# Hybrid encoder on one core: two column blocks of the output projection take the delta net's chunks first, and three scalings in the mixer run on ScalarE

## The chip, the core and the metric

The kernel runs on one core of a Trainium2 chip. The metric is the device time of one execution in microseconds (us), as the median of several runs. Each run's time covers the span from the first to the last instruction and a little around it.

## What is computed

Two layers of a bidirectional encoder on 256 tokens of width 2048, all in float32. A layer is a token mixer and a SwiGLU feed-forward net, each between two RMSNorms:

```python
h = rmsnorm(x, pre_mix_norm)
proj = h @ w_in                            # 2048 -> 4176 columns, for three groups
o_a = mla_mixer(...)                       # 8 heads of softmax attention, 1024 columns
o_b = conformer_conv(...)                  # GLU, depthwise conv of width 31, LayerNorm, swish, 512 columns
o_c = gdn_mixer(...)                       # gated delta net, 4 heads, two directions, 512 columns
mix = jnp.concatenate([o_a, o_b, o_c], axis=-1) @ w_out
x = x + rmsnorm(mix, post_mix_norm)
h = rmsnorm(x, pre_ffn_norm)
x = x + rmsnorm((silu(h @ w_gate) * (h @ w_up)) @ w_down, post_ffn_norm)
```

In `mla_mixer` the softmax weights are `exp(s - max) / sum`. In `gdn_mixer` the chunked delta rule multiplies the rows of several 128x128 matrices by gate values, one value for each row.

## The kernel before

Every large product is made from two float32r halves of each operand (`hilo`: the high half is a cast on ScalarE, line 333, and the low half a subtraction on VectorE, line 334). `dense` runs one product: for each 128-row chunk of the weights and each of the two token tiles it issues three matmuls of 512 columns (lines 358 to 360) into a PSUM bank named `acc`; there are four such banks, two for each product. It walks over units of two chunks. A unit loads 512 KB of weights through SP's queue into `ws` (5 buffers), splits them into `wh` and `wl` (5 buffers each), and then has twelve matmuls. At the end `evac` empties the two banks.

All small work of the mixer is background: attention of four head pairs (`attend`), the delta net (`gdn`), the convolution (`conformer`) and others are Python generators. After each unit `bg.step(1.6)` lets them go on; each step of a generator tells its cost at `yield`, and a unit's budget is 1.6. All but the convolution advance at most once in a unit. `bg.ensure` runs a generator to its end on the spot where a product needs its result. What is traced in this order is then put into each engine's queue by a planner, which fills an engine's gaps with later work that it takes to be ready. The 248 products of the depthwise convolution on VectorE (lines 951 and 954, one for each tap and each 128 channels, two layers) are such filling work. Each engine runs its own queue strictly in order.

The output projection has 16 chunks of rows: 0 to 7 are attention's (`oaT`), 8 to 11 the convolution's (`obT`), 12 to 15 the delta net's (`ocT`). It has four blocks of 512 columns. It runs in two passes, with the partial sums kept in SBUF between them:

```python
a, b = list(range(8)), [12, 13, 14, 15, 8, 9, 10, 11]
passes = [[a[:6], a, a, a], [a[6:] + b, b, b, b]]
```

So in the second pass block 0 takes chunks 6 and 7, then the delta net's four, and then at once the convolution's four. `need_mix` makes the convolution's generator end before its first chunk.

The end of the convolution is a chain: eight transposes of its sums (line 961), LayerNorm on VectorE (lines 964 to 969), eight transposes back (line 978), swish on ScalarE (line 983), and the split into halves (lines 333 and 334). The end of the delta net is eight transposes (line 918) and a split with a gain (lines 337 and 338).

The three scalings that change are: `kd` in `gdn_prep` (line 678, the delta net's keys by a gate), `vw` in `gdn_head` (lines 827 and 855, twice for each head and direction) and the division of the softmax weights by their sum in `attend` (line 1043, ahead of the transposes of line 1048). In `attend` the sum is inverted on VectorE (line 1041), after the exponentials on ScalarE (line 1037).

Of the kernel before, what the change touches and what calls it, by code (L numbers as in the profile page):

```python
# [9 lines left out]
F32 = mybir.dt.float32  # L10
# [6 lines left out]
P = 128  # L17
# [41 lines left out]
def kernel(  # L59
# [27 lines left out]
    def v3(ap, a):  # L87
        return ap.rearrange("p (a b) -> p a b", a=a)
# [250 lines left out]
                                 op0=ALU.mult, op1=ALU.subtract)  # L339
        return ins  # L340

    def dense(lhs, ks, n, load, evac, ch=2, need=None, pre=None, head=0, mid=None, tail=0,
              after0=None):

        acc = [psa.tile([P, 512], F32, tag="acc", name="acc") for _ in range(NT)]
        nu = -(-len(ks) // ch)
        held = []  # L350

        def mm(t, c, u, kc, wh, wl):
            i = u * ch + c
            rh = wh[:, c * n:(c + 1) * n]
            rl = wl[:, c * n:(c + 1) * n]
            xh, xl = lhs(kc[c], t)
            o = acc[t][:, 0:n]
            pe.matmul(o, xh, rh, start=(i == 0), stop=False)  # L358
            pe.matmul(o, xl, rh, start=False, stop=False)  # L359
            pe.matmul(o, xh, rl, start=False, stop=(i == len(ks) - 1))  # L360

        def unit(u):
            kc = ks[u * ch:(u + 1) * ch]
            m = len(kc)
            ws = wpool.tile([P, 1024], F32, tag="ws", name="ws", bufs=WSB)
            wv = ws[:, 0:m * n].rearrange("p (c n) -> p c n", c=m)
            load(wv, kc[0], m)
            wh = wpool.tile([P, 1024], F32R, tag="wh", name="wh", bufs=WHB)
            wl = wpool.tile([P, 1024], F32R, tag="wl", name="wl", bufs=WHB)
            with ExitStack() as order:  # L370
                if u < head:
                    for u0, ins in hold:
                        if u >= u0:
                            order.enter_context(tc.issue_after(ins.ins))
                hilo(wh[:, 0:m * n], wl[:, 0:m * n], ws[:, 0:m * n])
            if need is not None:
                for k in kc:
                    bg.ensure(*need(k))
            return u, kc, wh, wl

        for u in range(nu):
            a = unit(u)
            if head <= u < nu - tail:
                for c in range(len(a[1])):
                    for t in range(NT):
                        mm(t, c, *a)
            else:
                for c in range(len(a[1])):
                    mm(0, c, *a)
                held.append(a)  # L390
                if u == head - 1 and mid is not None:
                    mid()
                if u == nu - 1:
                    if pre is not None:
                        pre()
                        pre = None
                    evac(0, acc[0][:, 0:n])
                if u in (head - 1, nu - 1):
                    for h in held:
                        for c in range(len(h[1])):  # L400
                            mm(1, c, *h)
                    held.clear()
            bg.step(BUDGET)
        if pre is not None:
            pre()
        if after0 is not None:
            after0()
        for t in range(1 if tail else 0, NT):
            evac(t, acc[t][:, 0:n])

    def wload(w, n0, n):
# [102 lines left out]
    for l in range(DEPTH):  # L514
# [148 lines left out]
        def gdn_prep():  # L663

            nss = SM(16, "nss")
            kd, vk = [U(), U()], [U(), U()]
            for t in range(NT):
                for i, tl in enumerate((qT, kT)):
                    ps = TP()
                    junk = U()  # L670
                    for h in range(GH):
                        pe.transpose(ps[:, h * P:(h + 1) * P], hsl(tl, h, t), ident)
                    for h in range(GH):
                        j = i * 8 + t * 4 + h
                        act.activation(out=junk[:, h * P:(h + 1) * P], in_=ps[:, h * P:(h + 1) * P],
                                       func=AF.Square, accum_out=nss[:, j:j + 1])
                    if i:
                        dve.tensor_tensor(out=v3(kd[t], 4), in0=v3(ps, 4), in1=bc(G["eg5"][:, t, 1, t], 2, P),
                                          op=ALU.mult)
                    yield 0.4  # L680
            rn = rsqrt(nss, 1.0, EPS, 16, "rn")
            rk = rn[:, 8:16]

            b2, inr = SM(16, "b2"), SM(8, "inr")
            b24 = b2.rearrange("p (t d h) -> p t d h", t=NT, d=2)
            rk2 = SM(8, "rk2")
            dve.tensor_tensor(out=rk2, in0=rk, in1=rk, op=ALU.mult)
            dve.tensor_tensor(out=b24, in0=G["be4"], in1=bc(v3(rk2, NT), 2, 2), op=ALU.mult)
            dve.scalar_tensor_tensor(out=inr, in0=nss[:, 8:16], scalar=EPS, in1=rk, op0=ALU.add, op1=ALU.mult)
            nege = SM(8, "nege")  # L690
            for t in range(NT):
                dve.tensor_scalar(out=nege[:, t * 4:t * 4 + 4], in0=G["eg5"][:, 1 - t, 0, t], scalar1=-1.0,
                                  scalar2=None, op0=ALU.mult)
            yield 2.0

            for t in range(NT):
                ps = TP()
                for h in range(GH):
                    pe.transpose(ps[:, h * P:(h + 1) * P], hsl(vT, h, t), ident)
                dve.tensor_tensor(out=v3(vk[t], 4), in0=v3(ps, 4), in1=bc(inr[:, t * 4:t * 4 + 4], 2, P),  # L700
                                  op=ALU.mult)
                yield 0.7
            G.update(rn=rn, b24=b24, nege=nege, kd=kd, vk=vk)
# [72 lines left out]
        def gdn_head(h):  # L776
# [47 lines left out]
                m = 2 * (1 - d) + d  # L824
                pe.matmul(ps[:, d * P:(d + 1) * P], R[:, m * P:(m + 1) * P], vk[d][:, hs], start=True, stop=True)
            for d in range(2):
                dve.tensor_scalar(out=vw[:, d * P:(d + 1) * P], in0=ps[:, d * P:(d + 1) * P],
                                  scalar1=G["b24"][:, d, d, h:h + 1], scalar2=None, op0=ALU.mult)
            yield 0.4
            ps = TP()  # L830
            for d in range(2):
                pe.matmul(ps[:, d * P:(d + 1) * P], kd[d][:, hs], vw[:, d * P:(d + 1) * P], start=True, stop=True)
# [19 lines left out]
                pe.matmul(ps[:, d * P:(d + 1) * P], R[:, m * P:(m + 1) * P], S[:, (2 + d) * P:(3 + d) * P],  # L852
                          start=True, stop=True)
            for d in range(2):
                dve.tensor_scalar(out=vw[:, (2 + d) * P:(3 + d) * P], in0=ps[:, d * P:(d + 1) * P],
                                  scalar1=G["b24"][:, 1 - d, d, h:h + 1], scalar2=None, op0=ALU.mult)
            yield 0.4
            ps = TP()
            for t in range(NT):
                for d in range(2):  # L860
# [132 lines left out]
        def attend(hp, qn, kv):  # L993
# [28 lines left out]
            def head(i):  # L1022
# [17 lines left out]
                yield 0.8  # L1040
                dve.reciprocal(out=sm, in_=sm)
                for t in range(NT):
                    dve.tensor_scalar(out=pr[:, t * 256:(t + 1) * 256], in0=pr[:, t * 256:(t + 1) * 256],
                                      scalar1=sm[:, t:t + 1], scalar2=None, op0=ALU.mult)
                ps = TP()
                for kt in range(NT):
                    for t in range(NT):
# [1 line left out]
                                     pr[:, t * 256 + kt * P:t * 256 + (kt + 1) * P], ident)  # L1049
                pT = U()  # L1050
                act.copy(out=pT, in_=ps)
                yield 0.5
                ps = TP()
                for kt in range(NT):
                    pe.matmul(ps[:, 0:256], kv[kt][:, i * 256 + P:(i + 1) * 256],  # L1055
# [134 lines left out]
        def out_proj(lhs, passes, w, wpm, rname, need, after0):  # L1190
            parts = {}
            ssqp = [SM(4, "ssqp0"), SM(4, "ssqp1")]
            for i, ks in enumerate(passes):
                last = i == len(passes) - 1
                for nb in range(4):
                    if i == 0:
                        parts[(nb, 0)], parts[(nb, 1)] = U(), U()

                    def ev(t, ps):
                        o = parts[(nb, t)]  # L1200
                        if not last:
                            act.copy(out=o, in_=ps)
                            return
                        if i > 0:
                            dve.tensor_tensor(out=o, in0=o, in1=ps, op=ALU.add)
                            ps = o
                        junk = U()
                        act.activation(out=junk, in_=ps, func=AF.Square, accum_out=ssqp[t][:, nb:nb + 1])

                        def weigh():  # L1210
                            dve.tensor_tensor(out=o, in0=ps, in1=wpm[nb], op=ALU.mult)
                        if nb == 3:
                            residual(t, parts, ssqp, rname, weigh)
                        else:
                            weigh()
                    dense(lhs, ks[nb], 512, wload(w, nb * 512, 512), ev, need=need,
                          **(dict(tail=TAILG, after0=after0) if last and nb == 3 else {}))


        a, b = list(range(8)), [12, 13, 14, 15, 8, 9, 10, 11]  # L1220
        passes = [[a[:6], a, a, a], [a[6:] + b, b, b, b]]
        h2, F = {}, {}
        out_proj(lmix, passes, w_out[l], wpm, "rm", need_mix, lambda: norm_quad(0, 0, h2, (l, PRE_FFN)))

# [399 lines left out]
```

## Time and profile before

| what | value |
|---|---|
| runs before | median 2221.38 us of three (2218.79 to 2222.61) |
| the profiled execution, its own time | 2217.84 us |
| its span | 2216.0 us |
| PE (TensorE matmul) busy | 2183.0 us, 99% |
| DVE (VectorE) busy | 1916.4 us, 86% |
| ACT (ScalarE) busy | 1233.3 us, 56% |
| HBM read over the span | 402.94 MB, 183 GB/s |

The times of all rows are those of the profiled execution, and its own time lies 1.84 us above its span. In the profile a matmul is shown longer than the step from one matmul to the next, since matmuls are pipelined; so a gap between two matmuls of less than some 0.15 us shows as busy.

### The profile page before, as it was taken

The page shows a single profiled execution, that of the slowest core. Times are in us where ns is not written, and L with a number is a line of the kernel's source. Part 1 is how long each engine was busy: PE and PEld are TensorE (multiplying, and loading weights), DVE is VectorE, ACT ScalarE, POOL GpSimd, SP SyncE. Part 2 cuts the span into 40 slices and gives each one's busy share as a digit, 9 for nine tenths or more (in the row PEclk, how much of TensorE's full clock was granted, in tenths as well). Part 3 has the DMA queues.
Part 4 walks back from the last instruction along what each step waited for, and adds up shares of the span by engine and source line. Part 5 has one row for each costly group of instructions (what it writes and reads, how often), then busy time and mean ns, then how long its engine had stood idle before and what let it go on. Part 6 is the DMA issues. An engine that isn't in the chain of part 4 may idle for free.

```text
span 2216.0 us, 29534 instructions
## 1 busy us (share of the span) xinstructions
PE 2183.0 (99%) x10399; PEld 1823.9 (82%) x10399; DVE 1916.4 (86%) x3149; ACT 1233.3 (56%) x1726; POOL 45.7 (2%) x93
## 2 busy tenths in 40 slices
PE   8999999999999999999999999999999999999998
PEld 6988887788888888888879888877888888888886
DVE  6787998899989988889787779979998998988896
ACT  6665545555555555655556655455555555565553
POOL 2000000000000000000000000000000000000000
PEclk9999999999999999999999999999999999999999
DMA  7554534556655656466656545244556556564564
GB/s 252 172 182 144 186 104 153 162 171 199 212 196 200 210 198 225 154 208 211 200 181 184 181 142 175 96 154 162 189 192 227 188 194 226 188 211 161 203 218 148
DMA packets 218547, 407.76 MB, mean 184 GB/s; under 512 B 17607, under 2 KB 30065, under 8 KB 218400
## 3 DMA queue, kind: packets, MB, share of 16 engines
q1 hardware_dynamic: 215360, 397.72, 54.1%
q0 software_dynamic: 3008, 8.16, 1.4%
q8 instruction: 81, 1.33, 0.2%
q14 instruction: 66, 0.54, 0.1%
q10 hardware_dynamic: 32, 0.01, 0.0%
HBM read 402.94 MB, written 2.90 MB: 183 GB/s over the span
## 4 chain that ended last, share of the span: by engine, by line
PE 92%; DVE 5%; DMA 1%; ACT 1%; issue 0%; SPq 0%; DVEq 0%; ACTq 0%; POOLq 0%
PE acc L1398 19%; PE tp L1398 19%; PE tp L1525 10%; PE acc L1525 10%; PE acc L359 9%; PE acc L360 9%; PE acc L358 9%; DVE wl L334 1%; DVE xs L501 1%; PE acc L1246 1%; DMA ws<-in_w_in_dram 1%; PE tp L1055 0%; DMA cd<-u 0%; PE tp L808 0%; PE tp L801 0%; PE tp L1026 0%
## 5 line engine op out<-in xcount | busy, mean ns | idle before, releaser
L333 ACT CAST wh<-ws 128x1024 fp32r<-128x1024 f32 (+3 forms) x848 | 826.8, 997 | 742.5 <-DVE ws L1365 279.4
L334 DVE TENSOR_TENSOR wl<-ws,wh 128x1024 fp32r<-128x1024 f32 (+3 forms) x848 | 956.9, 1154 | 177.1 <-ACT wh L333 164.7
L358 PE MATMUL acc<-wh,u 128*128 128x512 f32 (+2 forms) x1088 | 419.7, 387 | 3.9 <-ACT u L333 3.4
L360 PE MATMUL acc<-wl,u 128*128 128x512 f32 (+2 forms) x1088 | 412.3, 380 | 5.3 <-DVE wl L334 5.1
L359 PE MATMUL acc<-wh,u 128*128 128x512 f32 (+2 forms) x1088 | 412.8, 380 | 1.4 <-DVE u L338 0.7
L1398 PE MATMUL acc<-wh,u 128*128 128x512 f32 x1220 | 376.3, 389 | 0.0
L1398 PE MATMUL tp<-wh,u 128*128 128x512 f32 x1220 | 375.8, 389 | 0.0
L1398 PEld LDWEIGHTS acc<-wh,u 128*128 128x128 f32 x1220 | 228.7, 188 | 47.8 <-DVE u L334 0.6
L1398 PEld LDWEIGHTS tp<-wh,u 128*128 128x128 f32 x1220 | 228.9, 188 | 47.5
L360 PEld LDWEIGHTS acc<-wl,u 128*128 128x128 f32 x1088 | 205.4, 189 | 42.1 <-DVE wl L334 7.7
L358 PEld LDWEIGHTS acc<-wh,u 128*128 128x128 f32 x1088 | 205.6, 189 | 40.1 <-ACT u L333 4.9
L359 PEld LDWEIGHTS acc<-wh,u 128*128 128x128 f32 x1088 | 205.7, 189 | 39.9 <-DVE u L338 3.4
L1398 PE MATMUL acc<-wl,u 128*128 128x512 f32 x610 | 237.3, 389 | 0.0
L1398 PE MATMUL tp<-wl,u 128*128 128x512 f32 x610 | 237.3, 389 | 0.0
L1525 PE MATMUL tp<-wh,u 128*128 128x512 f32 x676 | 209.6, 391 | 0.0
L1525 PE MATMUL acc<-wh,u 128*128 128x512 f32 x676 | 208.2, 389 | 0.0
L1525 PEld LDWEIGHTS acc<-wh,u 128*128 128x128 f32 x676 | 126.9, 188 | 26.3
L1525 PEld LDWEIGHTS tp<-wh,u 128*128 128x128 f32 x676 | 125.9, 188 | 25.4
L1398 PEld LDWEIGHTS acc<-wl,u 128*128 128x128 f32 x610 | 114.5, 188 | 23.7
L1398 PEld LDWEIGHTS tp<-wl,u 128*128 128x128 f32 x610 | 114.5, 188 | 23.7
L1525 PE MATMUL tp<-wl,u 128*128 128x512 f32 x338 | 132.0, 390 | 0.2 <-DVE wl L334 0.2
L1525 PE MATMUL acc<-wl,u 128*128 128x512 f32 x338 | 131.5, 389 | 0.0
(330 smaller groups left out, 2165.2 us busy)
## 6 DMA issues: line engine op xcount, KB each, us to landing
ws<-in_w_gate_dram SPq DMA_DIRECT2D x176, 512.0 KB, 5.0
ws<-in_w_up_dram SPq DMA_DIRECT2D x176, 512.0 KB, 4.8
ws<-in_w_down_dram SPq DMA_DIRECT2D x176, 512.0 KB, 5.3
ws<-in_w_in_dram SPq DMA_DIRECT2D x112, 512.0 KB, 4.5
ws<-in_w_out_dram SPq DMA_DIRECT2D x64, 512.0 KB, 3.6
ws<-in_w_ukv_dram SPq DMA_DIRECT2D x16, 512.0 KB, 3.6
ws<-in_w_uq_dram SPq DMA_DIRECT2D x16, 384.0 KB, 3.3
ws<-in_w_in_dram SPq DMA_DIRECT2D x10, 444.0 KB, 3.9
```

Of the source, the lines that this page charges most:

```text
L333: act.copy(out=hi, in_=src)
L334: dve.tensor_tensor(out=lo, in0=src, in1=hi.bitcast(F32), op=ALU.subtract)
L358: pe.matmul(o, xh, rh, start=(i == 0), stop=False)
L359: pe.matmul(o, xl, rh, start=False, stop=False)
L360: pe.matmul(o, xh, rl, start=False, stop=(i == len(ks) - 1))
L501: ins = dve.scalar_tensor_tensor(out=xv, in0=parts[(c, t)], scalar=r[:, 0:1], in1=xv, op0=ALU.mult, op1=ALU.add)
L1246: pe.transpose(pt[:, c * P:(c + 1) * P], hn[t][:, c * P:(c + 1) * P], ident)
L1398: pe.matmul(o, a, b, start=count[i] == 1, stop=count[i] == total[i])
L1525: pe.matmul(prod[i], a, b, start=count[i] == 1, stop=count[i] == total[i])
```

## The change

The second pass over the output projection is cut into six calls. Blocks 0 and 1 first take the delta net's chunks, one after the other, and then both take the convolution's. Their four PSUM banks stay open meanwhile. `dense` can now go on in banks that were opened before (`acc`, `first`, `last`). Blocks 2 and 3 keep the order that they had.

The three scalings become `activation` with `Identity` and a scale of one value for each partition: the one VectorE instruction of `kd` becomes four on ScalarE, the others are one for one. The cost that these steps report to the background drops: 0.4 to 0.0 after `kd` and after both `vw`, 0.5 to 0.2 after the softmax transposes.

```diff
-    def dense(lhs, ks, n, load, evac, ch=2, need=None, pre=None, head=0, mid=None, tail=0,
+    def dense(lhs, ks, n, load, evac, ch=2, need=None, pre=None, head=0, mid=None, tail=0, acc=None,
+              first=True, last=True,
               after0=None):
-        acc = [psa.tile([P, 512], F32, tag="acc", name="acc") for _ in range(NT)]
+        if acc is None:
+            acc = [psa.tile([P, 512], F32, tag="acc", name="acc") for _ in range(NT)]
...
-            pe.matmul(o, xh, rh, start=(i == 0), stop=False)
+            pe.matmul(o, xh, rh, start=(first and i == 0), stop=False)
             pe.matmul(o, xl, rh, start=False, stop=False)
-            pe.matmul(o, xh, rl, start=False, stop=(i == len(ks) - 1))
+            pe.matmul(o, xh, rl, start=False, stop=(last and i == len(ks) - 1))
...
-        for t in range(1 if tail else 0, NT):
+        for t in range(1 if tail else 0, NT if last else 0):
             evac(t, acc[t][:, 0:n])
...
                     if i:
-                        dve.tensor_tensor(out=v3(kd[t], 4), in0=v3(ps, 4), in1=bc(G["eg5"][:, t, 1, t], 2, P),
-                                          op=ALU.mult)
-                    yield 0.4
+                        for h in range(GH):
+                            act.activation(out=kd[t][:, h * P:(h + 1) * P], in_=ps[:, h * P:(h + 1) * P],
+                                           func=AF.Identity, scale=G["eg5"][:, t, 1, t, h:h + 1])
+                    yield 0.0
...
             for d in range(2):
-                dve.tensor_scalar(out=vw[:, d * P:(d + 1) * P], in0=ps[:, d * P:(d + 1) * P],
-                                  scalar1=G["b24"][:, d, d, h:h + 1], scalar2=None, op0=ALU.mult)
-            yield 0.4
+                act.activation(out=vw[:, d * P:(d + 1) * P], in_=ps[:, d * P:(d + 1) * P],
+                               func=AF.Identity, scale=G["b24"][:, d, d, h:h + 1])
+            yield 0.0
...
             for d in range(2):
-                dve.tensor_scalar(out=vw[:, (2 + d) * P:(3 + d) * P], in0=ps[:, d * P:(d + 1) * P],
-                                  scalar1=G["b24"][:, 1 - d, d, h:h + 1], scalar2=None, op0=ALU.mult)
-            yield 0.4
+                act.activation(out=vw[:, (2 + d) * P:(3 + d) * P], in_=ps[:, d * P:(d + 1) * P],
+                               func=AF.Identity, scale=G["b24"][:, 1 - d, d, h:h + 1])
+            yield 0.0
...
                 for t in range(NT):
-                    dve.tensor_scalar(out=pr[:, t * 256:(t + 1) * 256], in0=pr[:, t * 256:(t + 1) * 256],
-                                      scalar1=sm[:, t:t + 1], scalar2=None, op0=ALU.mult)
+                    act.activation(out=pr[:, t * 256:(t + 1) * 256], in_=pr[:, t * 256:(t + 1) * 256],
+                                   func=AF.Identity, scale=sm[:, t:t + 1])
...
                 act.copy(out=pT, in_=ps)
-                yield 0.5
+                yield 0.2
...
-            for i, ks in enumerate(passes):
+            kept = {}
+            for i, calls in enumerate(passes):
                 last = i == len(passes) - 1
-                for nb in range(4):
+                for n, (nb, ks) in enumerate(calls):
                     if i == 0:
                         parts[(nb, 0)], parts[(nb, 1)] = U(), U()
+                    opens = nb not in [c[0] for c in calls[:n]]
+                    closes = nb not in [c[0] for c in calls[n + 1:]]
+                    if opens and not closes:
+                        kept[nb] = [psa.tile([P, 512], F32, tag="acc", name="acc") for _ in range(NT)]
...
-                    dense(lhs, ks[nb], 512, wload(w, nb * 512, 512), ev, need=need,
+                    dense(lhs, ks, 512, wload(w, nb * 512, 512), ev, need=need, acc=kept.get(nb) if last else None,
+                          first=opens, last=closes,
                           **(dict(tail=TAILG, after0=after0) if last and nb == 3 else {}))
...
-        a, b = list(range(8)), [12, 13, 14, 15, 8, 9, 10, 11]
-        passes = [[a[:6], a, a, a], [a[6:] + b, b, b, b]]
+        a, b, d = list(range(8)), [8, 9, 10, 11], [12, 13, 14, 15]
+        passes = [[(0, a[:6]), (1, a), (2, a), (3, a)],
+                  [(0, a[6:] + d), (1, d), (0, b), (1, b), (2, d + b), (3, d + b)]]
```

## Rows read from the trace of the kernel before

**Rows 1.** The page's first part: busy us (share of span), instructions.

```profile
PE 2183.0 (99%) x10399; PEld 1823.9 (82%) x10399; DVE 1916.4 (86%) x3149; ACT 1233.3 (56%) x1726; POOL 45.7 (2%) x93
```

**Rows 2.** Waits of PE, whole span: waiter, releaser, us in total, times, longest.

```profile
PE acc L360 <- DVE wl L334: 5.1, 3, 1.7
...
PE acc L358 <- ACT u L333: 3.4, 3, 1.4
PE tp L1048 <- DVE u L1043: 3.2, 5, 1.3
```

**Rows 3.** Windows: stretch, length, busy PE, PEld, DVE, ACT, POOL; clock; DMA.

```profile
225.00:346.00 121.00, 119.40 (x680) 103.82 (x679) 119.18 (x292) 61.21 (x106) 5.23 (x7) 1.00 0.43 140
308.00:319.00 11.00, 9.49 (x51) 7.32 (x50) 10.87 (x29) 7.25 (x16) 0.00 (x0) 1.00 0.33 108
348.00:367.00 19.00, 17.02 (x83) 12.88 (x82) 15.88 (x42) 11.81 (x16) 0.00 (x0) 1.00 0.45 149
...
1446.00:1470.00 24.00, 21.98 (x98) 16.83 (x97) 16.98 (x43) 12.86 (x17) 0.00 (x0) 0.93 0.39 133
1464.00:1469.00 5.00, 5.00 (x16) 3.92 (x17) 1.02 (x2) 1.07 (x2) 0.00 (x0) 0.66 0.30 105
```

**Rows 4.** Windows, a stretch of the feed-forward net without gaps.

```profile
750.00:800.00 50.00, 50.00 (x222) 41.41 (x221) 45.68 (x57) 27.16 (x31) 0.00 (x0) 1.00 0.63 210
```

**Rows 5.** Timeline of layer 0, 348 to 367: start, us, what [idle before, releaser].

```profile
348.12 0.39 PE L360 MATMUL acc<-wl,u 128*128 128x512 f32 x1
...
348.61 1.26 PE L918 MATMUL tp<-ident,u 128*128 128x128 f32 x8
...
359.84 0.41 PE L978 MATMUL tp<-ident,u 128*128 128x128 f32 x2 [0.32 <-DVE sm L254]
...
359.99 1.28 ACT L983 ACT_TABLE_LOAD   x1
...
362.83 0.40 PE L360 MATMUL acc<-wl,u 128*128 128x512 f32 x1
...
364.64 1.20 PE L358 MATMUL acc<-wh,u 128*128 128x512 f32 x4 [1.42 <-ACT u L333]
```

**Rows 6.** Timeline of layer 1, PE, 1457 to 1470.

```profile
1462.50 1.19 PE L358 MATMUL acc<-wh,u 128*128 128x512 f32 x4 [1.42 <-ACT u L333]
...
1465.22 0.63 PE L358 MATMUL acc<-wh,u 128*128 128x512 f32 x1
...
1467.78 0.43 PE L358 MATMUL acc<-wh,u 128*128 128x512 f32 x1
```

**Rows 7.** Timeline of layer 0, DVE, 345 to 347: the convolution's last product.

```profile
345.68 0.47 DVE L954 SCALAR_TENSOR_TENSOR u<-u,cols 128x241 f32<-128x241 f32 x1
```

**Rows 8.** Timeline of layer 0, 313 to 317: the last softmax.

```profile
314.21 0.16 DVE L1041 RECIPROCAL sm<-sm 128x2 f32<-128x2 f32 x1
...
314.66 0.61 DVE L1043 TENSOR_SCALAR u<-u,sm 128x256 f32<-128x256 f32 x2
...
314.87 1.05 ACT L333 CAST wh<-ws 128x1024 fp32r<-128x1024 f32 x1
...
315.15 0.72 PE L1048 MATMUL tp<-ident,u 128*128 128x128 f32 x4 [1.25 <-DVE u L1043]
```

**Rows 9.** One line's view: count, ns min/median/max, first and last start in us.

```profile
L1043 DVE TENSOR_SCALAR u<-u,sm x32: 334/347/355, 188.8 to 1413.8; 128x256 f32<-128x256 f32 x32
```

**Rows 10.** Groups of lines on DVE and ACT, by shape: count, busy us, mean ns.

```profile
L337 ACT ACTIVATE u<-tp,cols 128x256 fp32r<-128x256 f32 x16 | 7.5, 471 | 8.8 <-DVE u L338 8.8
...
L846 ACT ACTIVATE u<-tp,sm 128x128 f32<-128x128 f32 x16 | 5.2, 365 | 2.3 <-DVE u L843 2.3
...
L855 DVE TENSOR_SCALAR u<-tp,sm 128x128 f32<-128x128 f32 x16 | 4.8, 344 | 0.3
L827 DVE TENSOR_SCALAR u<-tp,sm 128x128 f32<-128x128 f32 x16 | 4.3, 341 | 0.0
L678 DVE TENSOR_TENSOR u<-tp,sm 128x512 f32<-128x512 f32 x4 | 2.8, 688 | 1.7 <-ACT u L675 1.7
```

## Prediction

> **What bounds the kernel now.** I read the page's busy shares first. PE is busy for 2183.0 of 2216.0 us [rows 1], so 33.0 us of visible idle is nearly all that any change of order can win; the change adds and removes no matmul (the second pass has 6 + 4 + 4 + 4 + 8 + 8 = 34 chunks where it had 10 + 8 + 8 + 8 = 34). So the question is which waits of PE the change reaches. The list of PE's waits [rows 2] names two that belong to the mixer: the first matmul of a chunk (L358) waits for a split on ScalarE (L333), and the softmax transposes (L1048) wait for the division on VectorE (L1043), 3.2 us in five places. The longest, for `wl`, is behind the residual at the end of the projection and at the start of the kernel; nothing in the change touches it.
>
> The windows then say where. From 348 to 367 us, the start of the second pass in layer 0, PE is busy for 17.02 of 19 us; in layer 1 for 21.98 of 24 [rows 3]. That is 1.98 and 2.02 us of idle. The timeline shows its cause: the transposes of the normalized convolution wait 0.32 us, then the first matmul of chunk 8 starts at 364.64 after 1.42 us of idle, when the one before it had started at 362.83 [rows 5]. The wait is the end of a chain, in which a table load of 1.28 us on ScalarE for the swish [rows 5] stands too. Layer 1 has the same 1.42 us, and pays again behind it: six matmul steps from 1465.22 to 1467.78 take 2.56 us [rows 6], that is 0.427 us each against 50/222 = 0.225 us in an undisturbed stretch [rows 4]. The granted clock of those five microseconds is 0.66 [rows 3]: part of them is at the lower level (1.2 GHz), after the gap. The extra is 2.56 - 6 x 0.225 = 1.2 us; I count 1.5 us, since a few steps ahead of 1465.22 are slow as well.
>
> A second place is the last softmax of a layer. From 308 to 319 us PE is busy for 9.49 of 11 us [rows 3], so 1.51 us are lost, 1.25 of them in one wait for the division [rows 8].
>
> VectorE sets when the convolution ends. From 225 to 346 us it is busy for 119.18 of 121 us [rows 3], its gaps filled with the convolution's products, of which the last starts at 345.68 [rows 7]. So any VectorE work that leaves this stretch moves that end forward.
>
> **The change part by part.**
>
> *The order of the chunks.* Between the delta net's chunks of block 0 and the convolution's stand now the delta net's four chunks of block 1: 4 x 2 x 3 = 24 matmuls of 0.225 us [rows 4], 5.4 us of work that needs nothing new. The convolution's halves were ready some 364.6 - 363.1 = 1.6 us late for their matmul [rows 5]; the need moves by 5.4 us, so 3.8 us are left even if nothing else helps. The visible wait of 1.42 us in each layer goes. The 0.32 us ahead of L978 may stay, since PE takes its queue in order and that wait is for VectorE's chain, not for the chunk. The other idle of the window (1.98 - 1.74 = 0.24 us) and gaps too short to show are in the next paragraphs. With the low half late as well, I count 1.9 us for each layer: more than the two visible waits of 1.74 us, less than all of the window's 1.98. With the layer 1 clock loss: 2 x 1.9 + 1.5 = 5.3 us. The lower bound is 2 x 1.42 = 2.8 us (the clock falls anyway, and L978 still waits).
>
> What this costs: all four banks are taken until block 0 closes, so block 2 can open only when block 0's two banks are added up on VectorE. Two additions of 512 columns take some 2 x 0.69 us (an estimate from the equally large L678 [rows 10]); the 24 matmuls of block 1's convolution chunks hide it with 5.4 us. Without that cover it is at most 1.4 us a layer. I take nothing. The loads of weights are the same 17 units in another order on SP's queue: none is added, and none waits for something new.
>
> *VectorE relieved.* `kd` gives up 2 x 0.688 us in a layer, `vw` 16 x 0.34, the softmax 16 x 0.35 [rows 9, 10]: 1.4 + 5.5 + 5.5 = 12.4 us. In the stretch from 225 to 346 us lie all of `vw` and two of the four head pairs, 8 divisions (the others start at 188.8 [rows 9] and ahead of 225). Back to back, two instructions take 0.61 us where their means add to 0.69 [rows 8, 9]. So 5.5 + 2.7 = 8.2 us by the means, about 7 us by steps. The convolution's last product ends some 7 us sooner, and its chain follows. For block 0 that comes on top of the 5.4 us and buys nothing more. It does protect the gain of the order: together there are over 10 us of slack.
>
> *The reported costs.* A step of `vw` for four heads used to charge 4 x 0.4 = 1.6, a unit's whole budget, so nothing behind it advanced in that unit. Now it charges nothing. Going through the budget by hand, the delta net's last steps are traced one unit of twelve matmuls (2.7 us) earlier. Pass 2 opens with L918 at 348.61, where the matmul before it had started at 348.12 [rows 5]: 0.49 us against a step of 0.225, and the matmuls behind it come with similar small gaps. I take 0.5 us a layer, 1.0 in all, from 0 to 0.7 a layer.
>
> *ScalarE loaded.* It takes 8 `kd`, 16 `vw` and 16 softmax scalings a layer. From a bank, 128 columns with a scale for each partition take 0.365 us, 256 columns 0.471 (L846 and L337 [rows 10]). The sum is 24 x 0.365 + 16 x 0.471 = 16.3 us a layer for 12.4 us taken from VectorE. ScalarE is busy for 56% of the span [rows 1] and for 61.21 of 121 us in the crowded stretch [rows 3], so it has the room; the price is in order. The queue behind each new instruction holds the casts of the weights (L333), and PE waits for these. With five `wh` buffers four units, 4 x 12 x 0.225 = 10.8 us, are ahead of it, so a delay of one or two microseconds doesn't reach PE there. `kd` and `vw` stand in the delta net's chain, in which a unit of other matmuls lies between steps; I take nothing, and up to 1 us a layer as the bound.
>
> The softmax is the place that pays. Before, VectorE divided while ScalarE was done with the exponentials and went on to a cast of 1.05 us at 314.87 [rows 8]. Now the two scalings of a head, 2 x 0.471 = 0.94 us, follow on ScalarE where VectorE took 0.61 [rows 8]: 0.3 us later at the best. If the cast is put ahead of them, 1.05 more. PE waited here in 5 of 16 heads only [rows 2], so elsewhere other matmuls cover it. I take 0.5 us for each layer's last pair, 1.0 in all, from -3.0 (both waits of 1.5 us go) to +2.7 (cast and scaling in front, both layers).
>
> A rule of the Trainium skill speaks against this part. The page "ScalarE: Activation LUTs", section "Rules for kernel authors", says to multiply on VectorE and not on ScalarE. Rows agree that one costs more: 365 against 341 to 344 ns for 128 columns, 471 against 346 for 256 [rows 10, 9]. By the Trainium skill's formula (same page, section "What ACT_TABLE_LOAD costs"; one pointer operand, so 186 + 93 + 0.833 N ns) I estimate 386 and 492 ns, and the layer's sum would be 17.1 us where the rows give 16.3.
>
> **The sum.** 5.3 + 1.0 - 1.0 = 5.3 us less. The profiled execution's own 2217.84 becomes 2212.5. It lay 3.5 us under the median of the runs, 2221.38; carried over, the prediction is 2216.0 us. A measurement of this kernel tells some 0.2%, 4.4 us, from no change.
>
> **The rivals.**
>
> *All mixer waits go.* If the relieved VectorE also makes the softmax and the delta net's end prompt, 1.98 + 2.02 + 2 x 1.51 us of visible idle, the clock's 1.5 and small gaps of some 2 x 1.5 go: 11.5 us, so 2210. For it: VectorE is full in front of each of these waits [rows 3]. Against it: the softmax wait has ScalarE's work in its chain, and that grows.
>
> *The wait moves.* The convolution is now forced out two units later, so the planner may put its chain later by as much. Then PE meets L978, which it takes in order, as late as before, and the clock may fall behind another gap: 1.5 us gained, 2220. For it: PE waits for L978 already [rows 5]. Against it: the products end at 346 [rows 7] although most of them are traced only when the second pass, at 348, asks for the convolution; so they are filled in early whatever asks for them.
>
> *ScalarE becomes the chain.* In every softmax the cast stands in front and the two scalings follow, and a head's copy of its transposes stands in front of the other head's scalings: 1.05 + 0.33 us more, and 0.6 for the copy, some 2 us at 8 pairs, 16 us in all if nothing covers them. Less the 6.3 us won it gives up to 10 us more, 2231; it decides from 11 us on (1.3 us a pair), where the time is 0.2% above. For it: ScalarE's queue runs in order, and the copies and casts are in it already [rows 8]. Against it: PE waited in five of sixteen heads only [rows 2]. At some 6 us it would be a tie. The rule of the Trainium skill named above, taken at its word, leads here.
>
> **How the numbers follow.** The forecast has 0.45, all waits gone 0.20, the wait moved 0.23, ScalarE's chain 0.12. The likeliest one's own range is 2213 to 2219 (gain 2.8 + 0 - 0.5 to 5.3 + 1.4 + 1.5). The forecast lies at the edge of 0.2%: I give three quarters of it, 0.34, and all of the first rival to faster, together 0.54; 0.10 of the last rival to slower; the rest, 0.36, to the same. The range of eight in ten takes in the first rival with its bound and most of the second and stops ahead of the third: 2207 to 2223.
>
> **What would show it.** Right: no idle ahead of the first matmul of chunk 8 in the second pass, its swish and split done before PE gets there; no fall of the clock in layer 1 at this place; the last convolution product some 7 us earlier relative to the end of the first pass; L1048 waiting for ScalarE, a little longer than 1.25 us. Wrong: idle ahead of L978 or of block 2's first matmul; waits of L1048 in more than five heads; weights' casts that PE waits for; a fall of the clock elsewhere in the mixer.

## The result and the profile after

The change made the kernel slower: 2233.83 us median of six runs (2231.59 to 2236.35) against 2221.53 of six runs of the kernel before; the ratio is 1.0054, with a 95% interval of 1.0044 to 1.0064. That is 12.3 us more, where 5.3 us less had been forecast and the range ended at 2223.

In the page's first part PE is busy for 7.7 us more than in [rows 1] with the same number of matmuls. VectorE has 68 instructions fewer and ScalarE 80 more, which is what the three scalings make in two layers. Their busy times move by less than the prediction's sums: 16.5 us less on VectorE (24.8 by the sum for two layers) and 22.0 us more on ScalarE (32.6). Why they move by less is not isolated.

```profile
PE 2190.7 (98%) x10399; PEld 1827.0 (82%) x10399; DVE 1899.9 (85%) x3081; ACT 1255.3 (56%) x1806; POOL 45.6 (2%) x93
```

In the changed kernel lines 358 to 360 are 361 to 363, 918 is 922, 954 is 958, 961 is 965, 964 is 968, 978 is 982, 983 is 987, 1043 is 1047 and 1048 is 1052. PE's waits over the span of the changed kernel, in the columns of [rows 2]:

```profile
PE tp L982 <- DVE sm L254: 10.5, 2, 5.3
...
PE acc L361 <- ACT u L333: 2.6, 3, 1.1
```

No wait of the softmax transposes is left in the list ([rows 2] had 3.2 us). In its place stands a wait that [rows 5] showed with 0.32 us: the transposes of the normalized convolution wait 5.3 us, once in each layer. The windows of the changed kernel, columns as in [rows 3]:

```profile
225.00:346.00 121.00, 120.22 (x690) 104.73 (x689) 117.37 (x276) 68.40 (x129) 5.23 (x7) 1.00 0.44 141
308.00:319.00 11.00, 10.70 (x57) 8.73 (x57) 11.00 (x29) 8.50 (x21) 0.00 (x0) 1.00 0.16 49
345.00:360.00 15.00, 15.00 (x68) 12.42 (x67) 7.76 (x7) 6.54 (x8) 0.00 (x0) 1.00 0.64 209
360.00:365.00 5.00, 1.18 (x10) 0.85 (x8) 4.22 (x24) 2.34 (x2) 0.00 (x0) 1.00 0.41 132
365.00:370.00 5.00, 2.27 (x9) 1.50 (x9) 2.27 (x10) 1.76 (x4) 0.00 (x0) 0.59 0.22 84
370.00:375.00 5.00, 5.00 (x12) 3.94 (x13) 1.29 (x2) 1.42 (x3) 0.00 (x0) 0.50 0.00 0
```

From 345 to 360 us PE runs without a gap while VectorE is busy for only 7.76 of 15 us; then PE stands still for 6.55 of 10 us; then its clock is at the lower of its two levels (granted 0.50). PE's and then VectorE's and ScalarE's timelines of the changed kernel show the order:

```profile
359.91 0.39 PE L363 MATMUL acc<-wl,u 128*128 128x512 f32 x1
360.14 1.03 PE L965 MATMUL tp<-ident,u 128*128 128x128 f32 x8
366.45 0.66 PE L982 MATMUL tp<-ident,u 128*128 128x128 f32 x2 [5.27 <-DVE sm L254]
367.27 1.54 PE L982 MATMUL tp<-ident,u 128*128 128x128 f32 x6 [0.16 <-DVE u L973]
369.93 2.07 PE L361 MATMUL acc<-wh,u 128*128 128x512 f32 x4 [1.12 <-ACT u L333]
...
376.07 0.42 PE L361 MATMUL acc<-wh,u 128*128 128x512 f32 x1
```

```profile
331.80 0.46 DVE L958 SCALAR_TENSOR_TENSOR u<-u,cols 128x241 f32<-128x241 f32 x1
...
360.78 1.30 DVE L968 BATCH_NORM_STATS2 sm<-tp 128x6 f32<-128x512 f32 x2 [1.08 <-PE tp L965]
...
365.49 0.81 DVE L973 TENSOR_SCALAR u<-tp,sm 128x512 f32<-128x512 f32 x1
```

```profile
361.18 1.28 ACT L987 ACT_TABLE_LOAD   x1
368.21 1.02 ACT L987 ACTIVATE u<-tp,cols 128x256 f32<-128x256 f32 x2 [5.75 <-PE tp L982]
```

The convolution's last product ends at 332.3, and its first transposes run only at 360.1. Nothing held them up but their place in PE's queue: 72 matmuls of 512 columns stand between the delta net's transposes and these (before: none). What follows is the bare chain, with nothing of PE's work left behind it: the LayerNorm of the first 128 tokens until 366.3, then transposes, swish and split until 369.9. From 369.93 to 376.07 there are 14 matmul steps in 6.14 us, 0.44 us each where [rows 4] give 0.225: 3.0 us lost in layer 0. In layer 1 there are ten such steps, 2.2 us.

### The profile page after: what moved, and what is told of

Same layout as the page of the kernel before. It is cut to its first block, busy times and chain, and to the rows that moved or that the text cites. A ratio compares the mean times of both kernels' runs of the same rounds, so it can differ in the third digit from the quotient of the medians.

```text
span 2232.4 us, 29545 instructions
## 1 busy us (share of the span) xinstructions
PE 2190.7 (98%) x10399; PEld 1827.0 (82%) x10399; DVE 1899.9 (85%) x3081; ACT 1255.3 (56%) x1806; POOL 45.6 (2%) x93
```

## The experiments

Theory A, formed from this trace: the planner ranks work by the order in which it is traced. The convolution's tail is traced when its result is asked for (`bg.ensure`), and the new order asks for it after the very matmuls that were to hide it. Rivals: ScalarE's scalings lengthen the chains (B); four banks held open make block 2 wait (C). The table gives each kernel's ratio to the kernel before on the same chip, and the matmuls of 512 columns in PE's queue that stand behind the delta net's transposes ahead of the convolution's first eight ("to first"), and between these and its second eight ("first to second"), as the traces have them in layer 0.

| kernel | chunk order | convolution asked for | scalings on | to first | first to second | ratio (95%) |
|---|---|---|---|---|---|---|
| before | old | at its chunk | VectorE | 0 | 38 | 1 |
| changed | new | at its chunk | ScalarE | 72 | 0 | 1.0054 (1.0044 to 1.0064) |
| e1 | new | at its chunk | VectorE | 0 | 48 | 1.0016 (1.0007 to 1.0025) |
| e2 | old | at its chunk | ScalarE | 48 | 24 | 1.0012 (1.0004 to 1.0021) |
| e3 | new | pass start | ScalarE | 12 | 27 | 0.9976 (0.9967 to 0.9985) |
| e4 | old | pass start | ScalarE | 12 | 27 | 0.9973 (0.9962 to 0.9983) |
| e5 | new | ahead of block 1 | ScalarE | 48 | 24 | 1.0012 (1.0003 to 1.0021) |
| e6 | old | pass start | VectorE | 0 | 38 | 1.0002 (0.9993 to 1.0011) |
| e7 | old | pass start | ScalarE, old costs | 0 | 31 | 0.9983 (0.9974 to 0.9991) |
| e8 | old | pass start | VectorE, new costs | 3 | 50 | 1.0006 (0.9997 to 1.0015) |
| e11 | old | pass start | ScalarE for the softmax alone, old costs | 0 | 31 | 1.0008 (1.0000 to 1.0017) |
| e12 | old | pass start | ScalarE for the delta net alone, old costs | 0 | 30 | 0.9964 (0.9952 to 0.9977) |

**e1, the order alone.** The changed kernel with the scalings and costs of before:

```diff
-                act.activation(out=vw[:, d * P:(d + 1) * P], in_=ps[:, d * P:(d + 1) * P],
-                               func=AF.Identity, scale=G["b24"][:, d, d, h:h + 1])
-            yield 0.0
+                dve.tensor_scalar(out=vw[:, d * P:(d + 1) * P], in0=ps[:, d * P:(d + 1) * P],
+                                  scalar1=G["b24"][:, d, d, h:h + 1], scalar2=None, op0=ALU.mult)
+            yield 0.4
```

and likewise `kd`, the second `vw` and the softmax (cost 0.5 again).

> Only the new order of the chunks; the three scalings stay on VectorE and report their old costs. Theory A (the place in PE's queue: the planner ranks by the order of tracing, so the convolution's transposes stand behind all matmuls that are traced before them, and these no longer cover the chain): here the first eight transposes still fall into the gap at the delta net's end, as before, and 48 matmuls (10.9 us) cover the LayerNorm, but the second eight come last and 1.3 to 1.7 us of swish and split are bare in each layer, about what was waited for before. So within 3 us of before, 2218 to 2223. Theory B (ScalarE's scalings lengthen the chains): with none of them on ScalarE the loss is gone and the order's gain shows, 2213 to 2218. Theory C (four banks held open: block 2 waits for them): all of the loss is here, 2229 to 2236.

Measured: 2220.98 against 2217.21 us, 1.0016: neither the gain of theory B nor the loss of theory C, and a little more than theory A's estimate. Its timeline, and a window of it:

```profile
349.36 0.60 PE L965 MATMUL tp<-ident,u 128*128 128x128 f32 x4
...
361.25 1.03 PE L982 MATMUL tp<-ident,u 128*128 128x128 f32 x8
...
362.28 1.28 ACT L987 ACT_TABLE_LOAD   x1
...
365.30 1.08 PE L361 MATMUL acc<-wh,u 128*128 128x512 f32 x3 [3.02 <-ACT u L333]
...
365.00:370.00 5.00, 4.70 (x14) 3.69 (x15) 1.39 (x2) 1.79 (x4) 0.00 (x0) 0.66 0.27 95
```

The LayerNorm is covered. The second transposes stand behind all 48 matmuls, and then the table load, which I had not counted as bare, adds 1.28 us: PE waits 3.02 us where it waited 1.42. The clock falls behind that wait in layer 0 too: from 365 to 370 us it is granted with 0.66, where the kernel before has 1.00. So the new order by itself loses.

The count shows something more. The first matmul with a chunk of the convolution stands behind these same 48 matmuls in the kernel before. In the second pass blocks 0 and 1 have 60 matmuls that need nothing of the convolution (10 chunks of 6). In both kernels 12 of them stand ahead of the delta net's transposes and 48 behind, and all 60 ahead of the convolution's. VectorE's additions at the end of blocks 0, 1 and 2 show it in the kernel before:

```profile
370.62 1.37 DVE L1205 TENSOR_TENSOR u<-u,acc 128x512 f32<-128x512 f32 x2
...
375.64 1.34 DVE L1205 TENSOR_TENSOR u<-u,acc 128x512 f32<-128x512 f32 x2
...
386.50 1.36 DVE L1205 TENSOR_TENSOR u<-u,acc 128x512 f32<-128x512 f32 x2
```

Block 2 ends 10.9 us after block 1, which is its 48 matmuls; block 1 ends only 5.0 us after block 0, since its 24 for the delta net were done before. So the planner had put the order that the change writes down into PE's queue already: the new order by itself doesn't move the convolution's chunks at all, only the second transposes, from behind 38 matmuls to behind 48.

**e2, the scalings alone.** The changed kernel with the old order:

```diff
-                  [(0, a[6:] + d), (1, d), (0, b), (1, b), (2, d + b), (3, d + b)]]
+                  [(0, a[6:] + d + b), (1, d + b), (2, d + b), (3, d + b)]]
```

> Only the three scalings on ScalarE with their new costs; the chunks in the old order. Theory A: the first eight transposes stand behind 48 matmuls of the second pass, 24 matmuls (5.4 us) cover most of the LayerNorm chain of some 5.4 us, and the swish and split are bare: 1.5 to 2.5 us a layer where 1.74 were waited for before, less 3 us of softmax waits in both layers: 2216 to 2224. Theory B: the loss is here, 2229 to 2236. Theory C: faster than before by the softmax alone, 2216 to 2219.

Measured: 2220.69 against 2217.21 us, 1.0012. Against theory B, and theory A's place in the queue shows as two smaller waits; with the wait for the split they come to some 2.9 us a layer, more than the 1.5 to 2.5 expected. PE's waits in this kernel:

```profile
PE acc L361 <- ACT u L333: 3.3, 3, 1.4
PE tp L982 <- DVE sm L253: 1.7, 2, 0.9
PE tp L982 <- DVE u L973: 1.2, 2, 0.6
```

So neither half alone makes the whole loss: 0.0016 and 0.0012 alone, 0.0054 to 0.0058 together. With the old scalings the convolution's first transposes stand right behind the delta net's, with the new ones behind 48 matmuls, in the old order too. Here, too, all 60 matmuls of blocks 0 and 1 stand ahead of the convolution's (72 with the last 12 of the first pass), as in the changed kernel. My reading is that the planner put the first transposes into a gap that it foresaw on PE at the delta net's end, and that the new scalings closed that gap. This is argued and not shown: what the planner foresaw is in no trace, and PE waits for a moment at the delta net's end in the changed kernel as well (0.37 us).

**e3 and e4, the convolution asked for first.** One statement in `out_proj`, as the first of the loop over calls:

```diff
                 for n, (nb, ks) in enumerate(calls):
+                    if last and n == 0:
+                        bg.ensure("conf")
```

e3 has it on top of the whole change, e4 also has the old order of e2.

> The whole change, and the convolution's generator is run to its end at the start of the second pass, ahead of its first call, so that its transposes are traced before the matmuls that are to cover them. Theory A: the first transposes stand 12 matmuls behind the delta net's, 33 matmuls cover the LayerNorm and some 27 more the swish and split; no wait at either place, no fall of the clock: less than before by the waits there (5 us with the clock) and the softmax (3 us), 2210 to 2215. Theory B and theory C: the ask changes nothing that they name, 2229 to 2236.

> As the run before it (scalings on ScalarE, convolution asked for at the start of the second pass), but the chunks in the old order, so that the convolution's come 24 matmuls sooner. Theory A: the LayerNorm is covered by 31 matmuls, for swish and split only some 5 matmuls (1.1 us) are left: about 1 us of wait a layer, 2212 to 2217, 1 to 4 us over the run before it: that is what the order is worth by itself. Theory B: 2229 to 2236. Theory C: as the scalings alone, 2216 to 2219.

Measured: e3 2212.0 and e4 2211.59 against 2217.21 us. The same work, traced earlier, turns 1.0054 into 0.9976. That is 5.2 us less than before, where theory A had counted 8; what takes the rest stands under e12. Windows of e3, and its PE and ScalarE timeline:

```profile
345.00:370.00 25.00, 24.84 (x118) 20.41 (x117) 19.04 (x45) 15.26 (x22) 0.00 (x0) 1.00 0.51 179
1440.00:1475.00 35.00, 34.48 (x164) 28.19 (x163) 28.59 (x57) 21.09 (x31) 0.00 (x0) 1.00 0.51 177
```

```profile
342.82 0.66 PE L922 MATMUL tp<-ident,u 128*128 128x128 f32 x4 [0.36 <-DVE u L919]
...
346.98 1.04 PE L965 MATMUL tp<-ident,u 128*128 128x128 f32 x8
...
354.33 0.41 PE L982 MATMUL tp<-ident,u 128*128 128x128 f32 x2 [0.16 <-DVE sm L253]
354.38 1.28 ACT L987 ACT_TABLE_LOAD   x1
```

The chain starts 13 us earlier, PE is idle for 0.16 us of 25, and the clock stays at 1.00 in both layers. My expectation for e4 was wrong: it is not 1 to 4 us over e3 but level with it. In e4's queue the planner has itself put matmuls of block 1 behind the second transposes, ahead of block 0's first convolution chunk. Given a chain that is traced early, it finds the cover alone, as it did in the kernel before, and the new order is worth nothing here.

**e5, asked for one call later.** As e3, with `n == 1` in place of `n == 0`.

> The whole change, and the convolution asked for one call later than at the start of the second pass: after block 0's delta net chunks, ahead of block 1's. If the place in PE's queue sets the time (theory A), the loss lies between the two: the first transposes have the 24 matmuls of block 1 behind them (5.4 us) for a LayerNorm chain of some 5.4 us, swish and split are bare: 3 to 4 us of wait a layer as in the run with the scalings alone, so 1.000 to 1.003 of before. If the early ask helps for another reason (for one, that less is traced in a lump at the end), it helps here as much as at the start: 0.997 to 0.999.

Measured: 2220.31 against 2217.34 us, 1.0012, with e2's place in the queue and e2's waits, 2.8 us a layer where 3 to 4 were expected:

```profile
PE acc L361 <- ACT u L333: 3.1, 3, 1.4
...
PE tp L982 <- DVE sm L253: 1.7, 2, 0.8
PE tp L982 <- DVE u L973: 1.2, 2, 0.6
```

Asked for ahead of the first call, ahead of the second, or ahead of the third, as the change does, the same arithmetic takes 0.9976, 1.0012 and 1.0054 of before.

**e6, e7 and e8, which half pays.** The old order with the early ask: on the kernel before (e6), with ScalarE's scalings and the old costs (e7: `yield 0.4`, `0.4`, `0.4`, `0.5`), with VectorE's and the new costs (e8: `0.0`, `0.0`, `0.0`, `0.2`).

> The kernel before with nothing changed but the ask at the start of the second pass. Theory A: there the convolution's transposes already stand ahead of the second pass's matmuls, in the gap at the delta net's end, so the ask moves next to nothing: 0.999 to 1.001 of before, with the wait at the first convolution chunk and the softmax wait still there. Rival: the ask is what wins by itself, 0.997 or less.

> Old order, convolution asked for first, the three scalings on ScalarE, but with their old reported costs. If moving the work off VectorE is what makes the delta net and the softmax prompt: 0.997 to 0.998, as with the costs too. If the lower costs do it: about 1.000, with the softmax wait of 1.4 us in each layer still there.

> Old order, convolution asked for first, the scalings on VectorE, with the new reported costs alone. The counterpart of the run before it: about 1.000 if the engine does it, 0.997 to 0.998 if the costs do it (less 6 matmuls of cover behind the second transposes, so some 1 us of wait a layer at the first convolution chunk).

Measured: 2217.55, 2213.42 and 2218.32 against 2217.34 us. The ask alone changes nothing, since in the kernel before the transposes had their place already. The engine pays (0.9983, just short of the 0.997 to 0.998 expected), the costs alone do not. In e8 the costs removed the softmax wait but made another, 1.7 us of a second wait for `wl` in each layer:

```profile
PE acc L363 <- DVE sm L246: 3.4, 2, 1.7
```

**e9, PE kept busy while it waits.** The whole change, and behind the LayerNorm ten products that nobody reads:

```diff
                 yn.append(o)
                 yield 2.5
+            idle = TP()
+            for _ in range(10):
+                pe.matmul(idle[0:6, :], st, yacc[0], start=True, stop=True)
```

> The whole change, plus ten matmuls of 512 columns in float32 between the two sets of the convolution's transposes in PE's queue, whose result nobody reads: some 4 us of PE work where the change waits 5.3 us. No wait becomes shorter by it. If part of the loss is the clock that falls after the wait, the clock stays up here and the time falls by that part, some 2 to 3 us a layer: 1.002 to 1.004 of before. If the wait alone is the loss: no change, 1.005 to 1.006.

> The changed kernel as it is, beside the other runs on this chip: 1.0054 of before, 1.0044 to 1.0064.

Measured: 2234.51 and, for the change again (e10), 2233.8 against 2220.53 us: 1.0059 (1.0045 to 1.0073) and 1.0058 (1.0045 to 1.0070). By the wording of the expectation that would mean that the clock costs nothing, but the added work was twice as long as I had thought: 8.75 us. Timeline and window of e9, and the same window of the changed kernel:

```profile
361.13 1.03 PE L965 MATMUL tp<-ident,u 128*128 128x128 f32 x8
363.12 8.75 PE L979 MATMUL tp<-u,sm 128*6 128x512 f32 x20 [0.95 <-DVE sm L968]
...
374.22 0.96 PE L361 MATMUL acc<-wh,u 128*128 128x512 f32 x3 [1.32 <-ACT u L333]
...
365.00:376.00 11.00, 9.68 (x33) 3.57 (x31) 4.09 (x21) 3.18 (x6) 0.00 (x0) 1.00 0.15 48
```

```profile
365.00:376.00 11.00, 8.27 (x22) 6.22 (x23) 3.56 (x11) 3.29 (x7) 0.00 (x0) 0.54 0.10 38
```

From the first transposes to the first convolution chunk e9 takes 374.22 - 361.13 = 13.1 us, the change 369.93 - 360.14 = 9.8 us: 3.3 us more in each layer, and yet the same time. The clock is granted in full there, 1.00 against 0.54. So the lower clock costs the change about 3.3 us a layer, as much as the wait was lengthened by, give or take some 2 us a layer by the two intervals. The slow steps of the changed kernel's own trace, 3.0 and 2.2 us, agree with that.

**e11 and e12, which scaling pays.** The old order, the early ask and the old costs, with only the softmax division (e11) or only `kd` and `vw` (e12) on ScalarE.

> Old order and old costs, convolution asked for first, and only the softmax division on ScalarE. Theory: that wait is 1.5 us a layer and goes when the exponentials' own engine divides, so 3 us in all: 0.9983 to 0.9990. Rival: what helped is VectorE's relief as a whole, so that a third of it gives about 0.9995.

> The counterpart: only the delta net's two scalings on ScalarE. Theory: the delta net's end comes earlier and the convolution's wait gets cover, the softmax wait of 1.5 us a layer stays: 0.9990 to 1.0000. Rival (VectorE's relief as a whole): 0.9985.

Measured: 2222.6 and 2213.26 against 2220.53 us, the other way round from what I had thought. PE's waits for the softmax in e11, its ScalarE and PE timeline there, and the same wait in e12:

```profile
PE tp L1052 <- ACT u L1047: 5.4, 4, 1.9
...
316.81 1.70 ACT L1047 ACTIVATE u<-u,sm 128x256 f32<-128x256 f32 x4
...
317.38 1.74 PE L1052 MATMUL tp<-ident,u 128*128 128x128 f32 x8 [1.89 <-ACT u L1047]
```

```profile
PE tp L1052 <- DVE u L1047: 0.2, 1, 0.2
```

The division on ScalarE makes that wait 1.89 us where [rows 8] had 1.25; the delta net's scalings on ScalarE, with the division still on VectorE, let it vanish. e12 is the fastest of all, at 0.9964, but its interval overlaps those of e3 and e4. Why the softmax wait goes when the delta net's work moves, I have not isolated: the order of PE's queue around it changes as well.

The softmax on ScalarE also costs time at earlier head pairs, in gaps that the list of waits shows only in part. Windows of the kernel before, the changed kernel and e12 (columns as in [rows 3]):

```profile
180.00:240.00 60.00, 59.81 (x315) 51.96 (x314) 49.65 (x126) 36.07 (x67) 6.77 (x9) 1.00 0.41 122
180.00:240.00 60.00, 59.45 (x309) 50.84 (x308) 46.72 (x119) 37.57 (x73) 6.76 (x9) 1.00 0.41 120
180.00:240.00 60.00, 59.96 (x316) 52.09 (x315) 49.84 (x127) 35.75 (x66) 6.78 (x9) 1.00 0.43 124
```

PE starts 309 matmuls in the changed kernel where it started 315. Followed along PE's queue from its 900th matmul to its 1260th, transposes counted in (179 to 248 us before), this stretch takes 1.3 us more than in the kernel before, and 1.2 to 2.1 us more in every kernel here that divides on ScalarE; where VectorE divides (e1, e6, e8, e12) it doesn't take more. Layer 1 shows the same (1.3 us in the changed kernel). So the softmax's move costs the changed kernel and e3 some 2.6 us that e12 doesn't pay.

## Why the prediction was wrong

**The step that failed** is the first of the order of the chunks: "the need moves by 5.4 us, so 3.8 us are left even if nothing else helps". The need did not move. Between the delta net's transposes and the first matmul with a chunk of the convolution PE has 48 matmuls before and 48 in e1 with the new order alone; with the new scalings it has 72 in the old order (e2) and 72 in the new one (the change). The planner had drawn block 1's chunks of the delta net forward already, so the 1.42 us of wait were what was left with that cover in use. That e1 loses by itself (1.0016) shows that the sign of this term was wrong even without the other half.

What did move is the ask, and with it the tail's place in the queue. The prediction took the convolution's chain as starting when its data are there; it starts when PE reaches its transposes. In the change block 1's 24 matmuls, and all that is traced ahead of them, went in front of the chain and not beside it. e3 against the change shows it (one statement, 0.9976 against 1.0054), with e5 in between.

**VectorE relieved** was right in direction and too small by half: the last product ends at 332.3 and not at 346.2, 14 us sooner where about 7 were predicted. "Its chain follows" was the error. In the kernel before, too, the chain did not start with the last product: it ended at 346.2, and the first transposes ran 3.5 us later, behind the delta net's.

```profile
349.70 0.60 PE L961 MATMUL tp<-ident,u 128*128 128x128 f32 x4
```

With the new scalings they lose that place (e2), for the reason argued there.

**The reported costs**: the delta net's transposes start 6.2 us sooner (342.39 against 348.61 in [rows 5]), more than the 2.7 forecast. The 0.5 us a layer at their start was not won: a wait of 0.37 us stands there after the change, PE's list shows it as two waits of 0.7 us in all. The costs alone win nothing (e8).

**ScalarE loaded**: the bound held for the casts, since no long wait for `wh` appeared. The softmax term of +0.5 us a layer was too small for the move by itself: in e11 the longest wait is 1.89 us where it was 1.25, all of them together 5.4 us where [rows 2] had 3.2, and from 300 to 325 us the clock is granted with 0.93. In the whole change the last pair's wait is gone, 0.30 us of idle from 308 to 319 where [rows 3] had 1.51, but the earlier pairs cost 1.3 us a layer (under e12), which the prediction had put at nothing. The Trainium skill ("ScalarE: Activation LUTs", "Rules for kernel authors") says to multiply on VectorE. e11 agrees with that, e12 (0.9964) does not; VectorE was busy there for 119.18 of 121 us [rows 3]. That such a full engine counts for more than the price of one instruction is argued, since no run varies it by itself.

**Banks**: no wait of block 2; e3 and e4 are level.

**The clock**: it did not stay up; it fell in both layers, for about 3.3 us in each by e9, and 3.0 and 2.2 us by the slow steps in the trace.

**The rival that came true** is the second, "the wait moves": the planner puts the chain later, and PE meets L978 late. Its mechanism was named, with 0.23, but priced as the old wait, 2220. The sum with the measured terms: in each layer 6.55 us of wait and 3.3 us of clock, 19.7 us, for the old 5.0 (2 x 1.74 and 1.5); less 2.4 us of softmax waits: 12.3 us more. That this meets the measured difference to the tenth is luck. The 3.3 is known to some 2 us only, the sum leaves out the 2.6 us of the earlier head pairs, and the two traces from which its waits are read lie 16.4 us apart (spans of 2232.4 and 2216.0 us), since the profiled execution of the kernel before was a short one.

## What to carry to other kernels

Where a planner orders the queues, moving a consumer later also moves the request for its producer, and the producer's work then queues behind the cover that it was meant to have: ask for the producer first, then move the consumer. Before moving it, count in the trace what stands ahead of it in the engine's queue: here the planner had found the cover alone, and the move had nothing left to give. A producer's chain can also lose its place when other work around it changes (e2); look where its first instruction runs, and not only when its data are ready. For a chain, price not the wait that is seen, but its whole bare length if its start slips, with the lower clock behind it.

## What the runs showed of the hardware

The granted clock fell during a wait of 5.27 us and was 0.50 from 370 to 375 us in the changed kernel, with slow steps until 376; ten float32 products, whose result had no use, kept it at 1.00 through the same stretch in e9. In the kernel before, gaps of the same 1.42 us in both layers [rows 5, 6] were followed by full speed in one and by slow steps in the other (granted clock 1.00 and 0.93 in the windows around them, [rows 3]). A float32 matmul of 512 columns took two entries of some 0.43 us each in e9 (20 for ten), so it is nearly four times as long as a float32r one of 0.225 us.
